# Rotary products, modulation and retention transposes at other places of the order, and the loads of an overflow branch on another queue

## The chip, the core and the metric

The kernel runs on one core of a Trainium2 chip. The metric is the device time of one execution in microseconds; a run gives it as the median of several executions. Beside the times there is one profiled execution, from which all rows of a trace below are taken.

## What is computed

The reference is a transformer of two blocks over 256 tokens of width 1024, all in float32. The first block is the one that the change touches: a layer with modulation, three branches and a mixture of experts.

```python
mod = (jax.nn.silu(c) @ ada_w + ada_b)[:, None, :]
sh1, sc1, gt1, sh2, sc2, gt2 = jnp.split(mod, 6, axis=-1)
h = rmsnorm(x, norm1_g) * (1.0 + sc1) + sh1
(aq, ak, av, iq, ik, iw, bq, bf, bi, bg, cq, ck, cv, cg, ga, gb, gc) = split_cols(h @ w_in)
o_a = dsa_attention(...)
o_b = hgrn2(...)
o_c = retention(cq, ck, cv, cg)     # 4 heads; rotated q and k, decay, then norm and silu(cg)
merged = (jax.nn.sigmoid(ga) * (o_a @ w_branch_a)
          + jax.nn.sigmoid(gb) * (o_b @ w_branch_b)
          + jax.nn.sigmoid(gc) * (o_c @ w_branch_c))
x = x + gt1 * (merged @ w_out)
h2 = rmsnorm(x, norm2_g) * (1.0 + sc2) + sh2
x = x + gt2 * hier_moe(h2, ...)     # 32 experts, two per token
```

The second block has feed-forward layers, a gated spatial unit and one attention layer; the change leaves them alone.

## The kernel before, in words

Each float32 weight matrix is streamed from HBM in units of 128 x 2048 numbers (1 MiB) and split into two halves that TensorE takes as fp32r: `wh` is the rounded weight (a cast on ScalarE, line 259) and `wl` the rest (a subtraction on VectorE, line 260), twice per unit, for 128 x 1024 numbers each. The activations are split in the same way (`hi`, `lo`), and each product is three matmuls (lines 280 to 282). `load_split` does this for one unit and counts the units in `nunit`. There are three staging tiles for weights and three split halves, so the splits run a unit or two ahead of the matmuls. `block_a` multiplies two or four units into two PSUM banks, in groups of 12 matmuls of 512 columns for each unit and token half; `unit_b` is the other orientation, with 48 matmuls of 256 columns.

At the end of `load_split` two kinds of other work are given a turn. From the sixth unit on, every third unit takes one job of `self.jobs`: a step of the later modulation. For each of four chunks (`ada_jobs`: scale and shift of the second norm, then the two gates) there were five steps: step u loads 1 MiB of `ada_w` into the one tile `adw` and weighs it on VectorE, adds up the columns of step u - 1 (`sum_rows`: two matmuls, line 650, and a VectorE add, line 651); the last step also calls `done` for the finished columns. For a gate, `done` is `ada_row`: a transpose (line 677), a copy and a DMA. And every unit advances `self.steps` by one, which was the generator of the second branch's decay.

`hybrid` is the layer up to the experts, in this order: projections, first branch, cq and ck (units 40 to 47), `decay_out` of the second branch, the rotations of cq and ck (six VectorE products or sums each, lines 1089 to 1094), cv (units 48 to 55), cg into `oc` (units 56 to 63), the retention scores, `branch(32)` for the second branch (units 64 to 71), `retention` for the two token halves with its 16 transposes of two column blocks each (`t_split`, line 453, in the four PSUM banks "mm"), one early expert load, and `branch(36)` for the third (units 72 to 83). Then four units of the output projection. `b8` hands out nine work tiles of 8 KiB per partition.

`experts` then runs 16 pairs of experts. Their weights, 192 units of 1 MiB, are loaded by SyncE (`load_slot`, line 1222) into 17 slots, most of which become free as the layer before ends; a slot is loaded again as soon as TensorE has used it (`both`, matmuls at line 1241). After the eighth pair stands `overflow`: each engine loads a count into a register and passes `tc.If(n > C)` (line 1456). Its body, a loop over all experts, is for tokens that found no place among the 64 of an expert. The measured input has none, so the body does not run.

All instructions are written in program order and then ordered by a planner, which runs a timing model and puts an instruction on its engine's queue when its inputs are ready by that model; each engine works its queue in order. `no_sync(later, earlier)` tells the planner only that one instruction stays behind another.

Of the kernel before, what the change touches and what calls it, by code (L numbers as in the profile page):

```python
# [8 lines left out]
F32 = mybir.dt.float32  # L9
# [175 lines left out]
class Program:  # L185
    def __init__(self, tc, d, out, dbg=None, cap_limit=CAP):
        self.tc, self.nc, self.d, self.out, self.dbgs = tc, tc.nc, d, out, dbg or {}
        self.cap_limit = cap_limit
        self.flip = 0
        self.nhalf = 0  # L190
        self.whx = None
        self.res = self.edge = self.rest = None
        self.nfront = FRONT
        self.ready = []
        self.ahead = []
        self.jobs = []
        self.behind = None
        self.steps = iter(())
        self.nunit = 0

    def pad(self, pool, n, name):
# [38 lines left out]
    def load_split(self, ap, kt, n=2048, o=0):  # L240

        nc = self.nc
        ws = self.stage(ap, n)
        m, per, w = n // 2, kt // 2, n // kt
        behind = self.behind
        if self.nfront < FRONT:
            behind = self.fronts.get(1)
            self.nfront += 1
        parts = []
        for i in range(2):  # L250
            j = self.nhalf % (WHL + WH2 if self.whx else WHL)
            if self.whx and j >= WHL:
                wh, wl = [self.whx.tile([128, 1088], F32R, name=nm, bufs=WH2)[:, o:o + 1024] for nm in ("whx", "wlx")]
            else:
                whl = self.whl(F32R, j == WHL - 1, o)
                wh, wl = whl[:, :1024], whl[:, 1024:]
            src = ws[:, i * m:i * m + m]
            self.nhalf += 1
            w1 = nc.scalar.copy(wh[:, :m], src)  # L259
            w2 = nc.vector.tensor_sub(wl[:, :m], src, wh[:, :m].bitcast(F32))  # L260
            for ins, other in zip((w1, w2), behind or ()):
                if other is not None:
                    self.no_sync(ins, other)
            self.last_split = w1, w2
            parts.append((wh, wl))

        self.nunit += 1
        if self.jobs and self.nunit >= ADA_FROM and self.nunit % ADA_EVERY == 0:
            self.jobs.pop(0)()
        next(self.steps, None)  # L270

        def get(k, c0=0, c1=w):
            a = (k % per) * w
            return tuple(p[:, a + c0:a + c1] for p in parts[k // per])

        return get
# [26 lines left out]
    def block_a(self, aps, hi, lo, mid=None, between=None):  # L303


        ps = self.mms(2)
        last = 4 * len(aps) - 1
        for i, ap in enumerate(aps):
            w = self.weights(ap, 4, o=BESIDE if hi is self.hi else 0)
            for t in range(2):  # L310
                ts = slice(t * 128, t * 128 + 128)
                for k in range(4):
                    kk = i * 4 + k
                    self.mm3(ps[t], hi[:, kk, ts], lo[:, kk, ts], *w(k), kk == 0, kk == last)
                if i == 0 and t == 0 and between is not None:
                    between()
            if i == 0 and mid is not None:
                mid()
        return ps
# [123 lines left out]

        return tile_of

    def t_split(self, src, hi, lo, n, gain=None):

        nc = self.nc
        for i in range(0, n, 2):
            ps = self.mms().rearrange("p (a b) -> p a b", a=2)  # L450
            for j in range(2):
                for t in range(2):
                    nc.tensor.transpose(ps[:, j, t * 128:t * 128 + 128], src(i + j, t), self.ident)
# [199 lines left out]
    def ada_jobs(self, chunk, done):  # L653
# [4 lines left out]
        accs = {}  # L658

        def step(u):  # L660
            if u:
                self.sum_rows(accs[u - 1], o, chunk, u - 1)
            if u == 4:
                done(o)
                return
            ws = self.mix.tile([128, 2048], F32, name="adw", bufs=1)
            nc.sync.dma_start(ws, self.d["ada"][chunk * 4 + u])
            accs[u] = self.small.tile([128, 256], F32, name="acc", bufs=3)
            self.weigh_sum(ws, accs[u])

        return [lambda u=u: step(u) for u in range(5)]

    def ada_row(self, chunk, o):

# [54 lines left out]
    def hybrid(self):  # L729
# [79 lines left out]
        self.gemm_b(18, 4, lambda u, ps: self.evac(cq[:, u], ps))  # L809
        self.gemm_b(22, 4, lambda u, ps: self.evac(ck[:, u], ps))  # L810
        obs = self.decay_out(att, bi, ob)
        cqr, ckr = self.rotate(cq), self.rotate(ck)
        cv = [self.b8([128, 2048], name="cv") for _ in range(2)]
        self.proj_a(12, 4, lambda t, b, ps: self.evac(cv[t][:, b * 512:b * 512 + 512], ps))
        oc = [self.b8([128, 2048], name="oc") for _ in range(2)]
        self.proj_a(20, 4, lambda t, b, ps: self.silu_to(oc[t][:, b * 512:b * 512 + 512], ps))
        at = self.retention_scores(cqr, ckr)
        self.branch(32, obs, 4, mg, False)
        ocs = self.retention(at, cv, oc)
        self.no_sync(self.load_slot(), self.last_mm)  # L820
        self.branch(36, ocs, 8, mg, False, nk=4)
        self.dbg("mg", mg)
        while self.jobs:
            self.jobs.pop(0)()
# [6 lines left out]
        self.residual(acc, self.gt1)  # L831
        self.dbg("x1", self.x)

    def proj_a(self, off, nb, store):
        for b in range(nb):
            ps = self.block_a([self.d["w_a"][off + 2 * b], self.d["w_a"][off + 2 * b + 1]], self.hi, self.lo)
            for t in range(2):
                store(t, b, ps[t])
# [3 lines left out]
        self.nc.scalar.activation(s, ps, AF.Sigmoid)  # L842
        self.nc.vector.tensor_mul(out, ps, s)

    def branch(self, goff, o, woff, mg, first, nk=2):

        nc, d = self.nc, self.d
        sg = self.b8([128, 2, 1024], name="sg")
        self.proj_a(goff, 2, lambda t, b, ps: nc.scalar.activation(sg[:, t, b * 512:b * 512 + 512], ps, AF.Sigmoid))
        for b in range(2):  # L850
            ps = self.block_a([d["w_br"][woff + nk * b + i] for i in range(nk)], o[0], o[1])
            c = slice(b * 512, b * 512 + 512)
# [228 lines left out]


    def rotate(self, a):
        nc = self.nc
        cos = self.kk["cos"][:, None, :].to_broadcast([128, CH, S])
        sin = self.kk["sin"][:, None, :].to_broadcast([128, CH, S])
        e, o = a[:, :, 0], a[:, :, 1]
        tmp = self.b8([128, 2, CH, S], name="rot")
        nc.vector.tensor_mul(tmp[:, 0], o, sin)
        nc.vector.tensor_mul(tmp[:, 1], e, sin)  # L1090
        nc.vector.tensor_mul(e, e, cos)
        nc.vector.tensor_sub(e, e, tmp[:, 0])
        nc.vector.tensor_mul(o, o, cos)
        nc.vector.tensor_add(o, o, tmp[:, 1])
        return a

    def retention_scores(self, q, k):
        nc = self.nc
# [9 lines left out]
            nc.vector.tensor_mul(at[:, h, 256:], ps[:, 256:], dec[:, h, :128])  # L1108
        return at

    def retention(self, at, v, oc):
        nc = self.nc
        out = [(self.b8([128, 8, S], F32R, name="och"), self.b8([128, 8, S], F32R, name="ocl")) for _ in range(2)]
        for t in range(2):
            ms = self.small.tile([128, CH], F32, name="msc", bufs=2)
            rs = self.small.tile([128, CH], F32, name="rsc", bufs=2)
            pss = []
            for h in range(CH):
                hc = slice(h * 512, h * 512 + 512)
                ps = self.psum.tile([128, 512], F32, name="bg", tag="bg", bufs=4)  # L1120
                pss.append(ps)
                if t == 0:
                    nc.tensor.matmul(ps, at[:, h, :128], v[0][:, hc], start=True, stop=True)
                else:
                    nc.tensor.matmul(ps, at[:, h, 128:256], v[0][:, hc], start=True, stop=False)
                    nc.tensor.matmul(ps, at[:, h, 256:], v[1][:, hc], start=False, stop=True)
                jk = self.small.tile([128, 512], F32, name="sqj", bufs=1)
                nc.scalar.activation(jk, ps, AF.Square, accum_out=ms[:, h:h + 1])
            nc.vector.tensor_scalar(ms, ms, 1.0 / 512, EPS, op0=OP.mult, op1=OP.add)
            nc.gpsimd.tensor_tensor(out=rs, in0=ms, in1=self.mhalf[:, :CH], op=OP.pow)  # L1130
            for h in range(CH):
                hc = slice(h * 512, h * 512 + 512)
                nc.vector.scalar_tensor_tensor(oc[t][:, hc], pss[h], rs[:, h:h + 1], oc[t][:, hc], op0=OP.mult, op1=OP.mult)
        for z in range(2):
            self.t_split(lambda c, t: oc[t][:, (8 * z + c) * 128:(8 * z + c) * 128 + 128], out[z][0], out[z][1], 8)
        self.dbg("och0", out[0][0].bitcast(F32))
        self.dbg("och1", out[1][0].bitcast(F32))
        return Cat(out[0][0], out[1][0]), Cat(out[0][1], out[1][1])


    def experts(self):
# [304 lines left out]
    def overflow(self, topi, rgs, iota):  # L1446
# [1 line left out]
        nc, d, tc, exs = self.nc, self.d, self.tc, self.exs  # L1448
        C = self.cap_limit
        n = nc.values_load(topi[0:1, 0:1], min_val=0, max_val=S)  # L1450
        rg = self.dram.tile([NE, 128, 4], F32, name="rgscr")

        def mm():
            return self.psum.tile([128, 512], F32, name="mm", tag="mm", bufs=4)

        with tc.If(n > C):
            nc.sync.dma_start(rg.rearrange("e p c -> p e c"), rgs)
            with tc.For_i(0, NE) as e:
                with tc.tile_pool(name="ov", bufs=1) as ov:
                    r = ov.tile([128, 4], F32, name="r")  # L1460
                    nc.sync.dma_start(r, rg[ds(e, 1)].rearrange("a p c -> p (a c)"))

                    def weight(u, c):
                        w = ov.tile([128, 512], F32, name="ows")
                        nc.sync.dma_start(w, d["w_e"][ds(e, 1), u, :, c:c + 512].rearrange("a p c -> (a p) c"))
                        return w

                    for c0 in range(C, S, 128):
# [411 lines left out]
```

## Time and profile before

| | us |
|---|---|
| median of three runs | 2094.13 (2090.36 to 2094.59) |
| the profiled execution | 2091.0 |
| its span | 2089.2 |
| TensorE busy | 2020.9 |
| VectorE busy | 1111.5 |
| ScalarE busy | 844.4 |
| GpSimd busy | 25.1 |

503 MB were moved, 241 GB/s over the span. The profile lists what each engine did and, before each instruction, how long its engine was idle and what ended that. A busy time does not tell what a stage is worth: one reads for each stretch of the span which engine is full, and whether the chain of waits that ends last runs through it.

### The profile page before, as it was taken

To read this page: it belongs to the slowest core of one execution; us is meant where nothing else is said; L and a number is where in the kernel's file an instruction comes from. 1 tells how busy PE (TensorE), PEld (TensorE's weight loads), DVE (VectorE), ACT (ScalarE), POOL (GpSimd) and SP (SyncE) were. 2 spreads that over 40 slices of the span, in tenths; PEclk is the share of its full clock that TensorE was granted. 3 is DMA by queue.
4 is the path that set the end of the run, shared out by engine and by line. 5 is a ranking of instruction groups with operands and counts; after the bars stand their busy time and mean duration, and the time that the engine had idled before them with its cause. 6 is when DMAs were issued, how large, how long until landed. Compare 5 with 4: busy or idle time off the path is not lost.

```text
span 2089.2 us, 29415 instructions
## 1 busy us (share of the span) xinstructions
PE 2020.9 (97%) x12256; PEld 1605.2 (77%) x12256; DVE 1111.5 (53%) x1596; ACT 844.4 (40%) x1200; POOL 25.1 (1%) x40
## 2 busy tenths in 40 slices
PE   7999999999999999898889999999999999999998
PEld 5889889778784444343339998879999999989997
DVE  5887876755552011010027556666556655586555
ACT  3454335344442211111116445445444644475443
POOL 0000000000000000000000000000000000000000
PEclk9999999999999999999999999999999999999999
DMA  8655445565588999999995556544555455434552
GB/s 326 239 202 208 181 161 205 188 235 196 184 351 325 421 421 421 381 421 421 421 374 208 183 189 227 200 150 173 188 196 183 173 191 182 162 121 159 184 187 96
DMA packets 72124, 503.17 MB, mean 241 GB/s; under 512 B 8218, under 2 KB 10034, under 8 KB 11698
## 3 DMA queue, kind: packets, MB, share of 16 engines
q1 hardware_dynamic: 71986, 501.24, 62.9%
q8 instruction: 98, 1.61, 0.3%
q14 instruction: 40, 0.33, 0.0%
HBM read 500.14 MB, written 1.07 MB: 240 GB/s over the span
## 4 chain that ended last, share of the span: by engine, by line
PE 45%; DMA 9%; DVE 2%; issue 1%; ACT 1%; POOLq 0%; SPq 0%; DVEq 0%; POOL 0%; ACTq 0%
PE mm L280 10%; PE mm L281 10%; PE mm L282 10%; PE bg L280 5%; PE bg L281 5%; PE bg L282 5%; DMA wx<-in_w_e 3%; DMA we<-in_w_e 3%; DMA whl<-in_w_e 2%; DMA wp<-in_w_e 1%; PE mm L1241 1%; PE mm L423 0%; DVE sn L1803 0%; PE mm L1832 0%; DVE whd L260 0%
## 5 line engine op out<-in xcount | busy, mean ns | idle before, releaser
L260 DVE TENSOR_TENSOR whl<-ws,whl 128x1024 fp32r<-128x1024 f32 x228 | 277.8, 1221 | 220.3 <-ACT whl L259 219.1
L259 ACT CAST whl<-ws 128x1024 fp32r<-128x1024 f32 x228 | 238.3, 1048 | 294.4 <-PE mm L282 247.7
L260 DVE TENSOR_TENSOR wlx<-ws,whx 128x1024 fp32r<-128x1024 f32 x165 | 201.1, 1222 | 139.1 <-ACT whx L259 138.3
L259 ACT CAST whx<-ws 128x1024 fp32r<-128x1024 f32 x165 | 172.5, 1050 | 172.5 <-PE mm L282 97.0
L280 PE MATMUL mm<-hi,whl 128*128 128x256 f32 x836 | 235.4, 282 | 1.1 <-DVE whl L260 1.0
L281 PE MATMUL mm<-lo,whl 128*128 128x256 f32 x836 | 233.9, 280 | 0.1
L282 PE MATMUL mm<-hi,whl 128*128 128x256 f32 x836 | 233.3, 279 | 0.0
L260 DVE TENSOR_TENSOR whd<-ws,whd 128x1024 fp32r<-128x1024 f32 x113 | 137.8, 1219 | 110.4 <-ACT whd L259 109.6
L259 ACT CAST whd<-ws 128x1024 fp32r<-128x1024 f32 x113 | 118.2, 1046 | 171.3 <-PE mm L282 126.2
L280 PE MATMUL mm<-hi,wlx 128*128 128x256 f32 x640 | 178.7, 279 | 0.5 <-ACT rrow L1597 0.5
L281 PE MATMUL mm<-lo,whx 128*128 128x256 f32 x640 | 178.5, 279 | 0.0
L282 PE MATMUL mm<-hi,whx 128*128 128x256 f32 x640 | 178.5, 279 | 0.0
L280 PEld LDWEIGHTS mm<-hi,whl 128*128 128x128 f32 x836 | 157.2, 188 | 3.2 <-issue 1.2
L281 PEld LDWEIGHTS mm<-lo,whl 128*128 128x128 f32 x836 | 157.2, 188 | 1.5 <-DVE lo L621 0.7
L282 PEld LDWEIGHTS mm<-hi,whl 128*128 128x128 f32 x836 | 157.2, 188 | 0.2
L1261 DVE TENSOR_TENSOR act<-act,mm 128x512 f32<-128x512 f32 x16 | 11.0, 688 | 242.1 <-PE mm L1241 242.1
L280 PEld LDWEIGHTS mm<-hi,wlx 128*128 128x128 f32 x640 | 120.3, 188 | 1.8 <-ACT rrow L1597 0.8
L281 PEld LDWEIGHTS mm<-lo,whx 128*128 128x128 f32 x640 | 120.3, 188 | 0.7
L282 PEld LDWEIGHTS mm<-hi,whx 128*128 128x128 f32 x640 | 120.3, 188 | 0.0
L281 PE MATMUL mm<-whl,hi 128*128 128x512 f32 (+1 forms) x304 | 115.4, 379 | 0.0
L282 PE MATMUL mm<-whl,hi 128*128 128x512 f32 (+1 forms) x304 | 114.0, 375 | 0.0
L280 PE MATMUL mm<-whl,lo 128*128 128x512 f32 (+1 forms) x304 | 112.1, 382 | 1.5 <-DVE lo L437 1.5
(560 smaller groups left out, 4235.4 us busy)
## 6 DMA issues: line engine op xcount, KB each, us to landing
ws<-in_w_fi SPq DMA_DIRECT2D x88, 1024.0 KB, 4.8
we<-in_w_e SPq DMA_DIRECT2D x79, 1024.0 KB, 19.8
wx<-in_w_e SPq DMA_DIRECT2D x44, 1024.0 KB, 19.8
ws<-in_w_fo SPq DMA_DIRECT2D x44, 1024.0 KB, 4.8
ws<-in_w_a SPq DMA_DIRECT2D x40, 1024.0 KB, 4.8
ws<-in_w_e SPq DMA_DIRECT2D x33, 1024.0 KB, 19.8
ws<-in_w_b SPq DMA_DIRECT2D x26, 1024.0 KB, 4.8
whl<-in_w_e SPq DMA_DIRECT2D x22, 1024.0 KB, 17.0
```

Of the source, the lines that this page charges most:

```text
L259: w1 = nc.scalar.copy(wh[:, :m], src)
L260: w2 = nc.vector.tensor_sub(wl[:, :m], src, wh[:, :m].bitcast(F32))
L280: first = mm(out, ll, rh, start=start, stop=False)
L281: mm(out, lh, rl, start=False, stop=False)
L282: self.last_mm = mm(out, lh, rh, start=False, stop=stop)
L1241: self.chain(self.pe, self.nc.tensor.matmul(ps[j * 64:j * 64 + 64], xs[:, k, j], ws[j][:, o:o + 512], start=(k == 0), stop=(k == last)))
L1261: V.tensor_mul(a, a, ps[1])
```

## The change

There are four parts. The rotations become a generator, given to `self.steps`: one of their twelve operations per unit, held behind the unit's last VectorE split, over the units of cv and oc. `ada_jobs` has six steps for each chunk: `done` is a step of its own, one job after the last sum. `retention` is called once for each token half, the first ahead of `branch(36)`, the second between the two blocks of that branch's gate projection, followed by the early expert load; the transposes are a generator, `self.turns`, which `block_a` advances after each group of 12 matmuls: two empty turns, two turns of two column pairs, four of one. They use the four PSUM banks "bg". And the loads in the body of the overflow branch are issued by GpSimd instead of SyncE, with their scratch table laid out by partition.

```diff
-        self.steps = iter(())
+        self.steps = self.turns = iter(())
...
-        next(self.steps, None)
+        if (step := next(self.steps, None)) is not None:
+            self.no_sync(step, self.last_split[1])
...
                 if i == 0 and t == 0 and between is not None:
                     between()
+                next(self.turns, None)
...
-    def t_split(self, src, hi, lo, n, gain=None):
+    def t_split(self, src, hi, lo, n, gain=None, tag="mm"):
...
-            ps = self.mms().rearrange("p (a b) -> p a b", a=2)
+            ps = self.mms(tag=tag).rearrange("p (a b) -> p a b", a=2)
...
         def step(u):
+            if u == 5:
+                done(o)
+                return
             if u:
                 self.sum_rows(accs[u - 1], o, chunk, u - 1)
             if u == 4:
-                done(o)
                 return
...
-        return [lambda u=u: step(u) for u in range(5)]
+        return [lambda u=u: step(u) for u in range(6)]
...
-        cqr, ckr = self.rotate(cq), self.rotate(ck)
+        self.steps = (s for a in (cq, ck) for s in self.rotate(a))
         cv = [self.b8([128, 2048], name="cv") for _ in range(2)]
...
-        at = self.retention_scores(cqr, ckr)
+        for _ in self.steps:
+            pass
+        at = self.retention_scores(cq, ck)
         self.branch(32, obs, 4, mg, False)
-        ocs = self.retention(at, cv, oc)
-        self.no_sync(self.load_slot(), self.last_mm)
-        self.branch(36, ocs, 8, mg, False, nk=4)
+        ocs = self.retention_out()
+        part = [lambda t=t: self.retention(t, at, cv, oc) for t in range(2)]
+        part[0]()
+
+        def second():
+            part[1]()
+            self.no_sync(self.load_slot(), self.last_mm)
+            self.turns = self.retention_turns(oc, ocs)
+
+        self.branch(36, (Cat(ocs[0][0], ocs[1][0]), Cat(ocs[0][1], ocs[1][1])), 8, mg, False, nk=4, mid=second)
...
-    def proj_a(self, off, nb, store):
+    def proj_a(self, off, nb, store, mid=None):
         for b in range(nb):
+            if b == 1 and mid is not None:
+                mid()
...
     def rotate(self, a):
...
-        nc.vector.tensor_mul(tmp[:, 0], o, sin)
+        yield V.tensor_mul(tmp[:, 0], o, sin)
...
+    def retention_turns(self, oc, out):
+
+        yield
+        yield
+        for i, n in ((0, 2), (2, 2), (4, 1), (5, 1), (6, 1), (7, 1)):
+            for g in range(i, i + n):
+                z, c = divmod(2 * g, 8)
+                self.t_split(lambda j, t: oc[t][:, (2 * g + j) * 128:(2 * g + j) * 128 + 128], out[z][0][:, c:c + 2], out[z][1][:, c:c + 2], 2, tag="bg")
+            yield
...
-        rg = self.dram.tile([NE, 128, 4], F32, name="rgscr")
+        rg = self.dram.tile([128, NE, 4], F32, name="rgscr")
...
         with tc.If(n > C):
-            nc.sync.dma_start(rg.rearrange("e p c -> p e c"), rgs)
+            nc.gpsimd.dma_start(rg, rgs)
...
-                    nc.sync.dma_start(r, rg[ds(e, 1)].rearrange("a p c -> p (a c)"))
+                    nc.gpsimd.dma_start(r, rg[:, ds(e, 1)].rearrange("p a c -> p (a c)"))
...
-                        nc.sync.dma_start(w, d["w_e"][ds(e, 1), u, :, c:c + 512].rearrange("a p c -> (a p) c"))
+                        nc.gpsimd.dma_start(w, d["w_e"][ds(e, 1), u, :, c:c + 512].rearrange("a p c -> (a p) c"))
```

## Rows read from the trace of the kernel before

**Rows 1.** The page: TensorE's busy time; DMA share in 40 equal slices.
```profile
PE 2020.9 (97%) x12256; PEld 1605.2 (77%) x12256; DVE 1111.5 (53%) x1596; ACT 844.4 (40%) x1200; POOL 25.1 (1%) x40
...
DMA  8655445565588999999995556544555455434552
```

**Rows 2.** Stretches: us; busy us (instructions) per engine; granted clock, DMA share, GB/s.
```profile
363.00:380.00 17.00, 13.49 (x86) 12.15 (x85) 16.34 (x19) 6.04 (x10) 0.00 (x0) 0.90 0.50 178
380.00:519.00 139.00, 139.00 (x608) 111.28 (x607) 84.20 (x103) 61.55 (x79) 2.02 (x2) 1.00 0.58 211
519.00:531.00 12.00, 10.06 (x58) 8.07 (x57) 9.78 (x14) 7.09 (x11) 0.00 (x0) 1.00 0.69 262
...
639.00:845.00 206.00, 204.55 (x1036) 91.30 (x1036) 22.79 (x44) 42.33 (x77) 0.00 (x0) 1.00 0.99 411
...
870.00:885.00 15.00, 14.27 (x78) 6.80 (x80) 2.49 (x5) 4.30 (x8) 0.00 (x0) 1.00 0.73 287
885.00:1072.00 187.00, 168.91 (x796) 69.59 (x792) 16.40 (x32) 27.99 (x51) 0.00 (x0) 1.00 1.01 421
```

**Rows 3.** The chain of waits, 878 to 1080 us: start, us, what.
```profile
882.89 9.38 DMA wx<-in_w_e
...
1052.34 19.81 DMA whl<-in_w_e
...
1072.19 3.65 PE mm L1241 x14
```

**Rows 4.** Timeline of TensorE, 369 to 380: start, us, instruction, count, [idle before].
```profile
369.80 0.50 PE L650 MATMUL mm<-ones,acc 128*128 128x1 f32 x4
373.81 0.27 PE L677 MATMUL mm<-k,ada 128*8 128x128 f32 x1 [3.51 <-DVE ada L651]
...
374.99 0.63 PE L281 MATMUL mm<-whl,hi 128*128 128x512 f32 x1
...
378.33 0.39 PE L280 MATMUL mm<-whl,lo 128*128 128x512 f32 x1
378.56 0.40 PE L281 MATMUL mm<-whl,hi 128*128 128x512 f32 x1
```

**Rows 5.** A stretch inside that timeline, columns as in rows 2.
```profile
374.00:379.00 5.00, 5.00 (x16) 3.94 (x16) 5.00 (x6) 0.26 (x1) 0.00 (x0) 0.66 0.62 211
```

**Rows 6.** Timeline of VectorE, 360 to 392.
```profile
370.74 1.22 DVE L1091 TENSOR_TENSOR cq<-cq,k 128x1024 f32<-128x1024 f32 x1
...
373.61 0.15 DVE L651 TENSOR_TENSOR ada<-mm,cc 128x2 f32<-128x2 f32 x1
```

**Rows 7.** Timeline of TensorE, 524 to 532.
```profile
526.91 0.66 PE L453 MATMUL mm<-k,oc 128*128 128x128 f32 x4 [0.33 <-DVE sg L857]
528.65 0.66 PE L453 MATMUL mm<-k,oc 128*128 128x128 f32 x4 [1.08 <-DVE ocl L345]
529.85 0.66 PE L453 MATMUL mm<-k,oc 128*128 128x128 f32 x4 [0.54 <-DVE ocl L345]
```

**Rows 8.** Timeline of TensorE and VectorE, end of the second half of the retention.
```profile
482.93 1.02 PE L1126 MATMUL bg<-cv,attc 128*128 128x512 f32 x2
...
486.00 2.73 DVE L1133 SCALAR_TENSOR_TENSOR oc<-bg,rsc,oc 128x512 f32<-128x512 f32 x4 [1.12 <-POOL rsc L1130]
```

**Rows 9.** Line 1456, the conditional: duration in ns (min/median/max), first and last start.
```profile
L1456 SPq EVENT_SEMAPHORE  x8: 17/17/17, 878.9 to 881.8; - x8
L1456 POOLq COMPARE_BRANCH  x1: 45/45/45, 635.0 to 635.0; - x1
...
L1456 PEldq COMPARE_BRANCH  x1: 5912/5912/5912, 845.6 to 845.6; - x1
...
L1456 SPq COMPARE_BRANCH  x1: 50/50/50, 861.9 to 861.9; - x1
```

**Rows 10.** Timeline of the SyncE queue, 419 to 460 and 840 to 892.
```profile
440.23 1.96 SPq L1222 DMA_DIRECT2D wx<-in_w_e  x4
...
861.50 21.76 SPq L1222 DMA_DIRECT2D wx<-in_w_e  x4
```

More of the change, by code (lines that the diff above doesn't have):

```diff
@@ L843, in silu_to, with branch @@
         self.nc.vector.tensor_mul(out, ps, s)
-    def branch(self, goff, o, woff, mg, first, nk=2):
+    def branch(self, goff, o, woff, mg, first, nk=2, mid=None):
         nc, d = self.nc, self.d
         sg = self.b8([128, 2, 1024], name="sg")
-        self.proj_a(goff, 2, lambda t, b, ps: nc.scalar.activation(sg[:, t, b * 512:b * 512 + 512], ps, AF.Sigmoid))
+        self.proj_a(goff, 2, lambda t, b, ps: nc.scalar.activation(sg[:, t, b * 512:b * 512 + 512], ps, AF.Sigmoid), mid)
         for b in range(2):
@@ L1083, in rotate @@
     def rotate(self, a):
-        nc = self.nc
+        V = self.nc.vector
         cos = self.kk["cos"][:, None, :].to_broadcast([128, CH, S])
@@ L1088, in rotate @@
         tmp = self.b8([128, 2, CH, S], name="rot")
-        nc.vector.tensor_mul(tmp[:, 0], o, sin)
[L1090 to L1095, printed above, removed]
+        yield V.tensor_mul(tmp[:, 0], o, sin)
+        yield V.tensor_mul(tmp[:, 1], e, sin)
+        yield V.tensor_mul(e, e, cos)
+        yield V.tensor_sub(e, e, tmp[:, 0])
+        yield V.tensor_mul(o, o, cos)
+        yield V.tensor_add(o, o, tmp[:, 1])
     def retention_scores(self, q, k):
@@ L1109, in retention_scores, with retention_out, retention @@
         return at
-    def retention(self, at, v, oc):
+    def retention_out(self):
+        return [(self.b8([128, 8, S], F32R, name="och"), self.b8([128, 8, S], F32R, name="ocl")) for _ in range(2)]
+    def retention(self, t, at, v, oc):
         nc = self.nc
[L1113 to L1138, printed above, removed]
@@ new lines, in retention @@
+        ms = self.small.tile([128, CH], F32, name="msc", bufs=2)
+        rs = self.small.tile([128, CH], F32, name="rsc", bufs=2)
+        pss = []
+        for h in range(CH):
+            hc = slice(h * 512, h * 512 + 512)
+            ps = self.psum.tile([128, 512], F32, name="bg", tag="bg", bufs=4)
+            pss.append(ps)
+            if t == 0:
+                nc.tensor.matmul(ps, at[:, h, :128], v[0][:, hc], start=True, stop=True)
+            else:
+                nc.tensor.matmul(ps, at[:, h, 128:256], v[0][:, hc], start=True, stop=False)
+                nc.tensor.matmul(ps, at[:, h, 256:], v[1][:, hc], start=False, stop=True)
+            jk = self.small.tile([128, 512], F32, name="sqj", bufs=1)
+            nc.scalar.activation(jk, ps, AF.Square, accum_out=ms[:, h:h + 1])
@@ new lines, in retention @@
+        nc.vector.tensor_scalar(ms, ms, 1.0 / 512, EPS, op0=OP.mult, op1=OP.add)
+        nc.gpsimd.tensor_tensor(out=rs, in0=ms, in1=self.mhalf[:, :CH], op=OP.pow)
+        for h in range(CH):
+            hc = slice(h * 512, h * 512 + 512)
+            nc.vector.scalar_tensor_tensor(oc[t][:, hc], pss[h], rs[:, h:h + 1], oc[t][:, hc], op0=OP.mult, op1=OP.mult)
+    def retention_turns(self, oc, out):
[6 more added lines that the diff above has]
+            yield
```

## The prediction

> **What bounds the kernel now.** The page comes first: TensorE (PE) is busy 97% of the span, and the DMA engines have one long saturated stretch in the middle [rows 1]. So two things can shorten the run: PE's own gaps, and the DMA stream where that is full. The table by stage says which counts where [rows 2]. Before the experts PE is busy without a break, but for 363 to 380 us (13.49 of 17) and 519 to 531 (10.06 of 12); the DMA engines have room there (share 0.50 to 0.69). From 639 us they are full (411 to 421 GB/s, share 0.99 to 1.01), and only one later stretch falls below that: 870 to 885 us, at 287 GB/s. The chain of waits agrees: from 882.89 to 1072.14 us it runs through expert weight loads alone, in links of about 19.8 us, and after them through PE [rows 3]. In the expert stage, then, a microsecond in which no load runs is lost to the end, and PE's idle time there is worth nothing (168.91 busy of 187). In the stage before it a microsecond that PE stands is lost too: the expert stage starts with the routing that PE's work ends in, and moves with it.
>
> The profiled execution took 2091.0 us (span 2089.2 and 1.8 around it); the median of the three timed runs is 2094.13, 3.1 more. The sum is made against 2091.0, and its difference is taken off 2094.13.
>
> **Part 1: the modulation a step later.** A chunk's last column sum (two matmuls, L650, and a VectorE (DVE) add, L651) and what is done with the finished columns stood in one step; now the second follows three weight units later. In the trace that join is the 3.51 us gap: the sums of the gate start at 369.80, and the transpose L677 waits until 373.81 [rows 4]. What it waits for is the add at 373.61; it is short, but DVE's queue is in order, and ahead of it stand rotations and splits of some 1.2 us each [rows 6]. The wait has a tail: eight matmuls start between 374.99 and 378.33, 0.42 us apart, and the next two are 0.23 apart [rows 4]; the granted clock from 374 to 379 was 0.66, a mix of the 1.2 and the 2.4 GHz level [rows 5]. The tail is worth 3.34 - 8 x 0.23 = 1.5 us. A unit here is 24 matmuls, 24 x 0.23 = 5.5 us, and three are 16.6 us, so an add that is late by four is over by then. **Gain 3.5 + 1.5 = 5.0 us** (bounds: 0, if the planner puts the transpose behind such a queue again, and 5.0). The step adds no instruction. The jobs now end at unit 75 instead of 63, of 83 before the output projection, so nothing is left over for the end. The staging tile of the modulation is last used at unit 69, not 60. Four expert loads wait for its pool; they were issued at 440.23 [rows 10] and move back by 9 units of 5.5 us, to about 490. The DMA engines have 0.42 of their time free there [rows 2], and the loads are not read before 639: cost nothing. Without that cover (a release as late as the output projection) they would fall into the full stretch, at 19.8/8 = 2.5 us each [rows 3], 10 us.
>
> **Part 2: rotations bound to splits.** The same twelve DVE operations of about 1.2 us go out one to a unit, each behind the split of its unit, over 12 of the 16 units of cv and oc. From 363 to 380 DVE is busy 16.34 of 17 us, from 380 to 519 84.20 of 139 [rows 2], so there is room: 1.2 us more in each unit of 5.5. No PE wait but the one above is removed by it, and the gain of part 1 is not counted twice. It costs something if a user now waits. The scores need all rotations; these end at unit 59 and the scores are wanted after unit 63, 22 us later. And the second rotation buffer holds one of nine work buffers until unit 59, so the second oc tile, first written after unit 57, can be late by about two units; the four PSUM banks of the blocks allow two blocks to stand. I take nothing; the bounds are 0 and one wait like that of rows 4, 3.5 us.
>
> **Part 3: retention spread.** Before, the transposes of all oc tiles stood in front of the last branch, and PE waited three times for a bank to be emptied by DVE: 0.33 + 1.08 + 0.54 = 1.95 us [rows 7]. Now they are cut into six turns, between the groups of 12 matmuls (2.7 us) of the last branch, and use the other four banks. The first turn lies behind three groups, 8.2 us. What must be over by then is the second half of the retention; in the trace, from its last matmul's end at 483.95 to the end of the scaling at 488.73, it took 4.8 us [rows 8], and the planner had it over 41 us before the last of the transposes (488.73 against 529.85). So the cover is 3.4 us longer than the chain. Each later pair has one group or more between its transposes and its reader. What is late next is a split on ScalarE or DVE between two turns. **Gain 1.95, less 0.5** for one small wait left; bounds of what is left are 0 and six waits of the longest kind seen, 6 x 1.08 = 6.5 us.
>
> **Part 4: overflow loads by GpSimd.** The conditional is not taken here: no instruction of its body is in the trace. What it costs stands at L1456 [rows 9]. SyncE (SP) branches at 861.9, then eight semaphore instructions follow, the first at 878.9 and the last at 881.8, and only then the next load: four loads that otherwise leave one behind the other take from 861.50 over 21.76 us [rows 10], the first ahead of the branch. At 421 GB/s a load of 1 MiB takes 2.5 us, so a link of 19.8 us is eight loads in flight; the one issued at 861.5 lands at 861.5 + 19.8 = 881.3. I read this as a queue that has to see all its loads landed before it passes the conditional, since the body it skips would use the same eight counters. GpSimd (POOL), which had no work in the body, branches at 635.0 and has no such instructions: that is what SP becomes. GpSimd gets the eight, with nothing in flight, and nobody waits for it in this stage. The DMA hole is (1 - 287/421) x 15 = 4.8 us [rows 2], in the stretch where the chain is DMA. PE's own branch (5.91 us [rows 9]) stays; it lies beside full DMA. **Gain 4.8 us** (bounds 0 and 4.8).
>
> The Trainium skill says otherwise of such a wait ("Runtime: NRT & Kernel Launch", section on instruction fetch mechanics): a taken branch whose target lies outside what has been fetched stands until a DMA has brought the target. PE's 5.91 us at its branch agrees with that; that SP's first semaphore comes 17 us after its branch could be the same. By that rule the hole is gone too if SP's part of the body shrinks, and stays if SP still jumps over loop code.
>
> **Sum.** 5.0 + 1.45 + 4.8 = 11.25, taken as 11.2: 2091.0 - 11.2 = 2079.8 for a run like the profiled one, 2094.1 - 11.2 = **2082.9** by the median. I take 2082, since the before runs lie 3.8 below that median at their lowest.
>
> **Rivals.**
> - The hole at the conditional stays (SP still has semaphores of its own there, or waits for code). For: the branch is still on every engine's path. Against: GpSimd's row. 2094.1 - 6.45 = 2087.7.
> - The turns wait: at each of the six PE stands 1.08 us for a late split. 2094.1 - 9.8 + 6.5 - 1.95 = 2088.9. For: ScalarE and DVE also split weights then. Against: 380 to 519 us shows both with time to spare [rows 2].
> - The change doesn't do what it says: the planner keeps its own order, and the transpose of the gate waits again elsewhere. 2094.1 - 6.2 = 2087.9. For: the order is the planner's, by modelled times that missed this wait once. Against: three units between.
> - **Slower.** The turns' waits become long enough to take PE to the 1.2 GHz level. Place: the second block of gc and the first of the last branch. Price: six groups of 12 matmuls at 0.42 instead of 0.23 us are 13.7 us, with six waits of 1.08 us 20.2: 2094.1 - 9.8 + 20.2 = 2104.5. It decides from 14 us of such losses on (9.8 of gains and 4.2 of uncertainty). Against: the waits of rows 7 left the clock at 1.00 in that stretch [rows 2]; only 3.5 us in one piece lowered it.
>
> **How the numbers follow.** Forecast 0.70, hole stays 0.10, turns wait 0.10, planner's order 0.05, slower 0.05. A measurement of this kernel can tell about 0.2% (4.2 us) from no change: the bound is 2089.9. Faster by more: most of the forecast, the hole and the planner's case, half of the turns' case, less something for a second cost among those taken as nothing (3.5 us): 0.83. Within: 0.11. Slower: 0.06. The range reaches down to 2077 (the forecast on a run as low as the lowest before, with all 11.75 gained, is 2078.6) and up to 2090, which takes in three rivals.
>
> **What would show it.** Right: no PE gap before L677; no L453 waits in a row in front of the last branch; twelve rotations one to a unit; no semaphores of SP at the conditional, GpSimd with eight, and 420 GB/s straight through it; the expert stage starting some 6 us earlier and ending some 11 earlier. Wrong: a new PE wait for DVE near the oc units, L453 waits in the turns, or a DMA hole of 4.8 us that has only moved.

## The result, and the profile after

The kernel after took 2080.02 us (median, 2079.64 to 2080.85), the one before 2092.67 in the same rounds: a ratio of 0.9941, 95% interval 0.9929 to 0.9952. The profiled execution took 2079.64 (span 2078.0), 11.36 less than the 2091.0 of before; the sum of the prediction was 11.25. The total is right. Its terms are not: by the traces one was some 2 us too large and one too small by half, one part taken as nothing was worth something, and about a microsecond of the difference is no work of the change.

Busy shares on the page hardly move. The page of the kernel after, busy time of each engine, TensorE (PE) first:

```profile
PE 2018.9 (97%) x12256; PEld 1607.8 (77%) x12256; DVE 1110.5 (53%) x1596; ACT 843.9 (41%) x1200; POOL 25.4 (1%) x40
```

PE did the same work in 2 us less of listed time, and stood about 9 us less (2078.0 - 2018.9 against 2089.2 - 2020.9 [rows 1]; an engine stands while it waits with nothing to run, and a stand is one such wait). The table by stage of the kernel after shows where (columns as in [rows 2]):

```profile
363.00:380.00 17.00, 17.00 (x99) 14.98 (x98) 14.98 (x21) 7.95 (x11) 0.00 (x0) 1.00 0.50 185
...
519.00:531.00 12.00, 12.00 (x55) 9.89 (x54) 7.70 (x10) 5.51 (x7) 0.00 (x0) 1.00 0.66 252
...
863.00:878.00 15.00, 15.00 (x82) 6.95 (x83) 1.81 (x4) 4.30 (x8) 0.00 (x0) 1.00 1.01 418
878.00:1061.00 183.00, 167.58 (x794) 69.34 (x792) 16.38 (x32) 27.99 (x51) 0.00 (x0) 1.00 1.01 421
```

The two gaps of PE are closed (17.00 of 17, 12.00 of 12, where [rows 2] had 13.49 and 10.06), the clock of the first stretch is 1.00 instead of 0.90, and the stretch that ran at 287 GB/s runs at 418. The conditional has moved to L1478; its rows answer to [rows 9]:

```profile
L1478 POOLq EVENT_SEMAPHORE  x4: 17/43/43, 628.8 to 629.0; - x4
L1478 POOLq COMPARE_BRANCH  x1: 45/45/45, 626.3 to 626.3; - x1
L1478 POOLq INC_SWDGE_SEM  x1: 166/166/166, 629.1 to 629.1; - x1
...
L1478 PEldq COMPARE_BRANCH  x1: 5932/5932/5932, 837.3 to 837.3; - x1
...
L1478 SPq COMPARE_BRANCH  x1: 50/50/50, 853.5 to 853.5; - x1
```

SyncE (SP) has only its branch left. GpSimd (POOL) has five instructions behind its own, four semaphores and one of another kind, where the prediction had eight. The chain of the kernel after, in order of time (start, us, what), answers to [rows 3]:

```profile
839.24 21.30 DMA we<-in_w_e
...
860.61 19.82 DMA wx<-in_w_e
...
1039.59 21.27 DMA whl<-in_w_e
...
1060.89 3.65 PE mm L1263 x14
```

It is still one of expert loads, with no short link in it (the one of 9.38 us at 882.89 in [rows 3] is a load issued behind the hole, with few others in flight). The last load of the chain lands 11.3 us earlier (1060.86 against 1072.15). But the last link is 21.27 us long, where before it was 19.81; that comes back below.

For the experiments the span is cut at three places which every kernel has. For before and after the first two are the first and the last line of these fences (duration in ns, then first and last start in us); the line between them, the transposes of the second branch's output, parts stage A once more:

```profile
L877 PE MATMUL bg<-biasr,k x8: 592/592/697, 84.8 to 87.9; 128*128 128x512 f32 x8
...
L453 PE MATMUL mm<-k,ob x16: 271/272/273, 363.9 to 369.7; 128*128 128x128 f32 x16
...
L453 PE MATMUL mm<-k,mg x16: 270/272/273, 580.1 to 603.7; 128*128 128x128 f32 x16
```

```profile
L892 PE MATMUL bg<-biasr,k x8: 592/592/697, 83.8 to 86.9; 128*128 128x512 f32 x8
...
L455 PE MATMUL mm<-k,ob x16: 271/272/273, 361.8 to 367.7; 128*128 128x128 f32 x16
...
L455 PE MATMUL mm<-k,mg x16: 270/272/273, 571.2 to 594.8; 128*128 128x128 f32 x16
```

A is from the first bias product to the first transpose of the merged branches (parts 1 to 3 lie in it), B from there to GpSimd's branch (routing), C from there to the end of the span (part 4). What lies ahead of A is not touched by the change; it varied from 83.5 to 85.6 us over the profiled runs. Each stage is read from one profiled execution. The last column is the median against that of the kernel before in the same rounds.

| kernel | start | A | B | C | median | against before |
|---|---|---|---|---|---|---|
| before | 84.8 | 495.3 | 54.9 | 1454.2 | | |
| after | 83.8 | 487.4 | 55.1 | 1451.7 | 2080.02 | -12.65 |
| after, again | 83.8 | 487.1 | 55.1 | 1451.7 | 2080.22 | -11.37 |
| without 1 | 83.5 | 491.4 | 56.8 | 1451.4 | 2084.76 | -6.83 |
| without 2 | 83.9 | 490.1 | 54.9 | 1451.4 | 2082.78 | -8.81 |
| without 1, 2 | 85.0 | 492.8 | 56.8 | 1453.0 | 2086.78 | -4.81 |
| without 3 | 83.9 | 492.7 | 55.0 | 1451.4 | 2086.24 | -5.90 |
| without 3, eight banks | 84.8 | 487.1 | 54.9 | 1451.4 | 2079.89 | -12.52 |
| without 4 | 85.2 | 487.2 | 55.0 | 1454.0 | 2083.16 | -8.98 |
| SP store, 8 pieces | 85.6 | 487.3 | 54.9 | 1455.6 | 2084.47 | -7.67 |
| SP store, 1 piece | 84.3 | 487.2 | 55.1 | 1451.8 | 2079.74 | -12.40 |
| 1 and 2 alone | 84.4 | 490.8 | 55.1 | 1456.6 | 2089.45 | -2.96 |
| 3 alone | 85.5 | 492.3 | 55.1 | 1454.2 | 2087.95 | -4.46 |
| 4 alone | 84.2 | 496.8 | 54.9 | 1452.5 | 2089.00 | -3.41 |

Stage A repeats to 0.3 us in the five kernels that have parts 1 to 3 whole (487.1 to 487.4; differences in A are taken against 487.3 unless another kernel is named). Where TensorE stands in it, it repeats less well: three pairs of other kernels have the same code in A, and these differ by 1.5 (before, and 4 alone), 1.9 (without 3, and 1 and 2 alone) and 0.5 us (without 1 and 2, and 3 alone). The kernel before ran from 2090.4 to 2094.6, and the intervals of the ratios are 0.0018 to 0.0030 wide, that is two to three us to either side. So neither the stages nor the medians alone decide a difference of 1 or 2 us; both are given where they differ.

Stage A has a part ahead of the waits that the prediction priced: from the first bias product to the first transpose of the second branch's output it is 278.7 to 279.3 us in the five kernels without part 1, and 277.8 to 278.5 in the nine with it. The rest of A is 216.2 us before and 209.4 after.

### The profile page after: what moved, and what is told of

The parts are those of the page before. It is cut to its first block, busy times and chain, and to the rows that moved or that the text cites. A ratio compares the mean times of both kernels' runs of the same rounds, so it can differ in the third digit from the quotient of the medians.

```text
span 2078.0 us, 29416 instructions
## 1 busy us (share of the span) xinstructions
PE 2018.9 (97%) x12256; PEld 1607.8 (77%) x12256; DVE 1110.5 (53%) x1596; ACT 843.9 (41%) x1200; POOL 25.4 (1%) x40
## 4 chain that ended last, share of the span: by engine, by line
PE 82%; DMA 13%; DVE 3%; ACT 1%; issue 1%; POOLq 0%; SPq 0%; DVEq 0%; POOL 0%; ACTq 0%
PE mm L281 17%; PE mm L282 16%; PE mm L283 16%; PE mm L1263 8%; PE bg L281 5%; PE bg L282 5%; PE bg L283 5%; DMA we<-in_w_e 4%; DMA wx<-in_w_e 4%; DMA whl<-in_w_e 2%; PE bg L1025 1%; DMA ws<-in_w_e 1%; DMA wp<-in_w_e 1%; PE mm L1198 1%; PE bg L581 1%
## 6 DMA issues: line engine op xcount, KB each, us to landing
we<-in_w_e SPq DMA_DIRECT2D x79, 1024.0 KB, 19.8
wx<-in_w_e SPq DMA_DIRECT2D x44, 1024.0 KB, 19.8
ws<-in_w_e SPq DMA_DIRECT2D x33, 1024.0 KB, 19.8
whl<-in_w_e SPq DMA_DIRECT2D x22, 1024.0 KB, 19.8
```

## Experiments

### Parts 1 and 2: the wait ahead of the gate's transpose

Without part 1:

```diff
-            if u == 5:
-                done(o)
-                return
             if u:
                 self.sum_rows(accs[u - 1], o, chunk, u - 1)
             if u == 4:
+                done(o)
                 return
...
-        return [lambda u=u: step(u) for u in range(6)]
+        return [lambda u=u: step(u) for u in range(5)]
```

> Part 1 undone, the rest of the changed kernel kept: the finished columns of the modulation are used in the same step as their last sum again; the rotations stay one to a unit. The changed kernel took 2080.0 us, the one before 2092.7. Theory A (the join was late only because dense rotations stood ahead of the add on VectorE; either edit alone removes that): no stand of TensorE over 1 us ahead of the gate's transpose, 2080 within 1 us. Theory B (the later step is what removes it, as the prediction put it: a split of about 1.2 us each still stands ahead of the add): the 3.5 us stand and up to 1.5 us of clock tail return, 2083.5 to 2085.

It took 2084.76 us, 4.5 more than the changed kernel in the same rounds, and A is 4.1 longer. The timeline of TensorE in that kernel:

```profile
371.29 0.27 PE L679 MATMUL mm<-k,ada 128*8 128x128 f32 x1 [2.02 <-DVE ada L653]
```

The stretch behind it (columns as in [rows 2]):

```profile
372.00:374.00 2.00, 2.00 (x7) 1.52 (x6) 1.97 (x4) 0.00 (x0) 0.00 (x0) 0.50 0.80 334
```

And the timeline of VectorE (DVE) ahead of the add:

```profile
368.20 1.23 DVE L260 TENSOR_TENSOR whd<-ws,whd 128x1024 fp32r<-128x1024 f32 x1 [1.83 <-ACT whd L259]
369.35 1.22 DVE L1103 TENSOR_TENSOR rot<-cq,k 128x1024 f32<-128x1024 f32 x1
370.48 0.68 DVE L358 COPY ck<-mm 128x512 f32<-128x512 f32 x1
371.08 0.15 DVE L653 TENSOR_TENSOR ada<-mm,cc 128x2 f32<-128x2 f32 x1
```

The wait is back, and shorter: one rotation and a copy stand between the split at 368.20 and the add, where in the kernel before two rotations (369.61 and 370.74), a split and a copy did. Behind it the clock is at 0.50, that is 1.2 GHz. (B is 1.7 us longer in this execution, at a mean clock of 0.88 from 611 to 640, where the kernel after has 0.94; that is not tied to part 1, since the kernels before, 3 alone and 4 alone lack it too and have 54.9 to 55.1.) So thinning out VectorE alone does not remove the join (theory A falls). Without part 2:

```diff
-        self.steps = (s for a in (cq, ck) for s in self.rotate(a))
+        for a in (cq, ck):
+            for _ in self.rotate(a):
+                pass
```

> Part 2 undone, the rest of the changed kernel kept: the twelve products and sums of the rotations stand together again ahead of the third projection; the modulation stays a step later. Theory A and theory B (the later step alone removes the wait at the gate's transpose): 2080 within 1 us. Rival C (twelve dense operations of 1.2 us, about 14.6 us of VectorE, make the weight splits behind them late, and TensorE stands for those): one or more stands of TensorE for VectorE between 360 and 385 us of 1 us or more in sum, 2081 to 2085.

2082.78 us, and A is 2.8 us longer than with all parts. No wait at the transpose, but two others, in TensorE's list of waits (line waited for: us in total, times, longest):

```profile
PE mm L282 <- DVE whd L260: 1.1, 1, 1.1
PE mm L282 <- DVE whl L260: 1.0, 1, 1.0
```

And the stretch in which they lie:

```profile
363.00:380.00 17.00, 15.06 (x90) 12.75 (x88) 17.00 (x20) 7.42 (x9) 0.00 (x0) 1.00 0.33 121
```

That is the rival: with dense rotations VectorE is busy 17.00 of 17 us, and now splits of weights come late. In the kernel before these waits did not show; as I read it (no run tests it by itself), the 3.5 us for which TensorE stood gave VectorE the time to catch up. With both parts undone (the two diffs together):

> Parts 1 and 2 undone together, parts 3 and 4 kept. Prediction's sum: the stand of 3.5 us ahead of the gate's transpose and the stretch of 1.5 us lost at 0.66 of the clock return, 2085.0. Theory A: u1 and u2 are both at 2080 and only this one is at 2085. Theory B: u1 is here too. Rival (the wait was an accident of the other parts' order): no stand, 2080.

2086.78 us: A is 5.5 longer than after, and the wait of 3.5 us is there again:

```profile
PE mm L679 <- DVE ada L653: 3.5, 1, 3.5
```

Undone together they cost 5.5 in A, 4.2 of it behind the transposes of the second branch's output (213.6 against 209.4), where the wait lies; from there part 1 alone brings 2.7 and part 2 alone 1.4 (4.0 and 2.0 by the medians). (The profiled execution with both undone is the longest of nine, 2.5 us over their median; what it has over is in B and C.) So neither is the other's spare: they work on one queue. One thing the runs do not separate: with six steps to a chunk the gate's own last sum also comes later (its add at 394.20, the transpose at 415.9 in the kernel after), out of the stretch in which it waited.

> The changed kernel unaltered, timed in the same rounds as the three kernels with parts undone, so that differences of 1 to 5 us can be told: 2080, that is 0.9941 of the kernel before (interval so far 0.9929 to 0.9952). In its trace the stages up to 84 units should begin where they did: the expert stage 8.4 us earlier than in the kernel before, its last load 11.3 us earlier.

It did (2080.22; A 487.1).

### Part 3: other banks or other places

```diff
-        def second():
-            part[1]()
...
+        part[1]()
+        for z in range(2):
+            self.t_split(lambda c, t: oc[t][:, ...], ocs[z][0], ocs[z][1], 8)
+        self.no_sync(self.load_slot(), self.last_mm)
-        self.branch(36, ..., nk=4, mid=second)
+        self.branch(36, ..., nk=4)
```

> Part 3 undone, the rest of the changed kernel kept: both halves of the retention and all 16 transposes stand ahead of the last branch again and use the first four banks. Prediction's sum: TensorE stands for VectorE between the transposes, 1.95 us in three pieces before, so the expert stage starts 1.5 to 2 us later and the time is 2082. Rival (the stands are made up for elsewhere, or the turns cost as much): the expert stage starts at the same time, 2080 within 0.7 us.

2086.24 us, and 5.4 us more in A: neither forecast's number. The timeline of TensorE without part 3:

```profile
522.43 1.97 PE L455 MATMUL mm<-k,oc 128*128 128x128 f32 x8 [2.28 <-DVE ocl L347]
...
525.48 0.63 PE L282 MATMUL mm<-whl,hi 128*128 128x512 f32 x1
525.90 0.63 PE L283 MATMUL mm<-whl,hi 128*128 128x512 f32 x1
```

And a stretch of it:

```profile
523.00:527.00 4.00, 4.00 (x16) 3.61 (x15) 2.61 (x5) 1.17 (x2) 0.00 (x0) 0.50 0.02 8
```

The three short waits of [rows 7] have become one of 2.28 us, and the clock behind it is at 1.2 GHz: matmuls start 0.42 us apart, and the eight transposes take 1.97 us. Whether the place of the transposes or the banks matter was tried with the transposes written at that same place, and both sets of banks in turn:

```diff
-            self.t_split(lambda c, t: oc[t][:, ...], ocs[z][0], ocs[z][1], 8)
+            for c in range(0, 8, 2):
+                self.t_split(lambda j, t: oc[t][:, ...], ocs[z][0][:, c:c + 2], ocs[z][1][:, c:c + 2], 2, tag=("mm", "bg")[c // 2 % 2])
```

> As the kernel with part 3 undone (all transposes ahead of the last branch), but the pairs of columns take the banks mm and bg by turns, eight instead of four. That kernel took 2086.2 us, with a stand of 2.28 us behind 16 transposes and ten matmuls 0.43 us apart behind it. Theory B (TensorE waits for a bank to be emptied; other banks alone are enough, the spreading is not needed): no stand, 2080 to 2081. Theory P (it waits for VectorE's queue whatever the bank, so only spreading helps): the stand and the tail stay, 2085 to 2087.

2079.89 us, as fast as the changed kernel. Its transposes, from TensorE's timeline:

```profile
520.21 0.60 PE L455 MATMUL mm<-k,oc 128*128 128x128 f32 x4
520.65 0.38 PE L455 MATMUL bg<-k,oc 128*128 128x128 f32 x2
520.87 0.60 PE L455 MATMUL mm<-k,oc 128*128 128x128 f32 x4
521.30 0.60 PE L455 MATMUL bg<-k,oc 128*128 128x128 f32 x4
```

And the stretch around them:

```profile
519.00:531.00 12.00, 12.00 (x63) 10.16 (x63) 8.85 (x13) 5.49 (x8) 0.00 (x0) 1.00 0.36 138
```

No wait. TensorE waited for a bank to be emptied, and a second set of banks is enough; the turns between the groups of the last branch are not needed for it. (The order on the queue is not quite the same: with eight banks the planner put 16 of the 32 transposes into the first group, at 513.2 to 514.8 us, where without part 3 it had put eight. How much of the gain is that was not tried apart.)

### Part 4: what SyncE waits for at the conditional

```diff
-            nc.gpsimd.dma_start(rg, rgs)
+            nc.sync.dma_start(rg.rearrange("e p c -> p e c"), rgs)
...
-                        nc.gpsimd.dma_start(w, ...)
+                        nc.sync.dma_start(w, ...)
```

> Part 4 undone, the rest of the changed kernel kept: the loads in the body of the conditional, which does not run, are issued by SyncE again. Prediction's sum: SyncE gets eight semaphore instructions some 17 us after its branch, the load behind it is issued about 20 us after the one ahead of it, the DMA rate falls below 300 GB/s for about 15 us, and 4.4 to 4.8 us come back: 2084.4 to 2084.8. Rival (the hole costs nothing since TensorE's work is what ends last): 2080 within 0.7 us, hole in the trace all the same.

2083.16 us. (The scratch table has its old layout again here; the next two kernels keep the new one.) Without part 4 the row of SP at the conditional, its queue's timeline, the stretch behind it, and two links of the chain, each in a fence of its own:

```profile
L1478 SPq EVENT_SEMAPHORE  x8: 17/17/17, 871.2 to 874.1; - x8
```

```profile
853.73 21.81 SPq L1244 DMA_DIRECT2D wx<-in_w_e  x4
```

```profile
863.00:878.00 15.00, 14.11 (x78) 6.51 (x76) 2.50 (x5) 4.30 (x8) 0.00 (x0) 1.00 0.73 288
```

```profile
884.48 20.70 DMA we<-in_w_e
...
1044.60 19.81 DMA whl<-in_w_e
```

Wait and hole are as predicted. The price is less by the trace, 2.3 us in C; by the medians it is 3.1 against the kernel after. Then the two readings of the wait. SP's part of the body is a short store, with no loop, in eight transfers or in one:

```diff
-            nc.gpsimd.dma_start(rg, rgs)
+            for g in range(0, NE, 4):
+                nc.sync.dma_start(rg[:, g:g + 4], rgs[:, g:g + 4])
```

> The changed kernel, but the store of the scratch table in the body of the conditional is issued by SyncE in eight pieces; the loads of the body's loop stay with GpSimd, so SyncE's part of the body is short and has no loop. The body does not run. Drain theory (a queue that passes a conditional whose body uses its counters has to see the eight loads in flight landed): eight semaphore instructions of SyncE, the first about 17 us after its branch, a DMA hole of 4.4 to 4.8 us, 2084.4 to 2084.8. Fetch theory (the time went into fetching code that lies far away): no stand and no hole with such a short body, 2080 within 0.7 us. The Trainium skill (Runtime: NRT & Kernel Launch, instruction fetch mechanics) would give the second.

2084.47 us. The first three views again, with eight transfers:

```profile
L1478 SPq EVENT_SEMAPHORE  x8: 17/17/17, 871.5 to 874.4; - x8
...
L1478 SPq COMPARE_BRANCH  x1: 45/45/45, 854.5 to 854.5; - x1
```

```profile
854.12 21.68 SPq L1244 DMA_DIRECT2D wx<-in_w_e  x4
```

```profile
863.00:878.00 15.00, 14.15 (x76) 6.55 (x74) 2.50 (x5) 4.30 (x8) 0.00 (x0) 1.00 0.73 291
```

```diff
-            nc.gpsimd.dma_start(rg, rgs)
+            nc.sync.dma_start(rg, rgs)
```

> As the kernel with eight pieces, but the store of the scratch table is one transfer of SyncE, so one counter of the eight is used in the body. The body does not run. Drain theory: one semaphore instruction of SyncE, which waits for the one load on that counter alone: if that is the oldest of the eight in flight, about 2.5 us, the time of one load at 421 GB/s, and no hole, 2080 to 2080.7; if it is the youngest, about 17 us and a hole as with eight. Fetch theory: no stand, 2080 within 0.7 us.

2079.74 us. The same three with one transfer:

```profile
L1478 SPq COMPARE_BRANCH  x1: 50/50/50, 853.6 to 853.6; - x1
L1478 SPq EVENT_SEMAPHORE  x1: 17/17/17, 855.7 to 855.7; - x1
```

```profile
853.27 10.37 SPq L1244 DMA_DIRECT2D wx<-in_w_e  x4
```

```profile
863.00:878.00 15.00, 14.15 (x76) 6.50 (x74) 2.51 (x5) 4.30 (x8) 0.00 (x0) 1.00 1.01 419
```

Eight transfers in a body that never runs bring back eight semaphores, 17 us of wait and the hole; one transfer brings one semaphore, 2.1 us behind the branch, and no hole. Loads leave every 2.5 us and take 19.8, so 17 us fits the drain of all eight in flight, and 2.1 us that of the oldest. By these three kernels what counts is how many transfers of SP the body holds, not the length of its code: eight short transfers cost the same wait as the loop of loads. Nor is it the layout of the scratch table, which is the new one in both.

The rule of the Trainium skill which the prediction set against this reading ("Runtime: NRT & Kernel Launch", instruction fetch mechanics) gives no stand for so short a body, if that lies within what has been fetched, which no row shows; the row with eight transfers, beside the one with a single transfer, speaks against it for SP. PE's 5.9 us at its branch stay in all kernels (5.91 to 6.21 us); no run here tells whether that is the fetch.

### Each part alone

The kernel before with one part made, composed of the diffs above.

> Parts 1 and 2 alone (parts 3 and 4 undone). With all four parts the kernel took 2080.0 to 2080.2 us, the one before 2091.6 to 2092.7. Theory S (the parts add up; undoing parts 1 and 2 cost 6.6 us by the medians, 4.3 by the stage from the transposes of the second branch's output to those of the merged branches, 216.2 us before): 2085.5 to 2088, that stage 211.9. Theory I (they don't: with parts 1 and 2 the transposes ahead of the last branch come with one stand of 2.28 us and a slow clock behind it, as in the kernel with part 3 alone undone, where before there were three short ones): the stage about 214.9, 2088.5 to 2090.

A is 4.5 us shorter than before. The stand of 2.28 us is there, as theory I has it, but without a slow clock behind it in this execution. TensorE's timeline and the same stretch:

```profile
523.60 1.25 PE L455 MATMUL mm<-k,oc 128*128 128x128 f32 x8 [2.28 <-DVE ocl L347]
```

```profile
523.00:527.00 4.00, 3.40 (x19) 2.69 (x20) 3.60 (x7) 1.17 (x2) 0.00 (x0) 1.00 0.13 55
```

The stage that the theories name is 212.3 us, close to theory S (211.9); the median (2089.45) agrees with theory I. So this run does not decide between them. C is 2.4 us longer than before in the profiled run; an expert load near the end (`whl`) is issued 417.6 us behind GpSimd's branch, against 417.3 before, so the other 2 us lie later, behind the experts for the most part, and I can't say why.

> Part 3 alone (parts 1, 2 and 4 undone). Theory S (undoing part 3 cost 6.1 us by the medians, so doing it alone gives as much): 2086. Theory I (without the other parts only the three stands of rows 7 are there to be removed, and the stage goes from 216.2 to 213.6, as the kernel with parts 1 and 2 undone showed): 2089 to 2090. In both the stand of 3.5 us ahead of the gate's transpose is there.

3.0 us in A, 4.5 by the medians: between the two theories. Theory I's stage is met (213.6), with a median a microsecond better. Of the 3.0, 1.95 are the three stands and 0.4 lies ahead of the second branch's transposes; the rest was not located.

> Part 4 alone (parts 1 to 3 undone). Prediction's sum: 4.8 us less than the kernel before, 2087.2. By the traces so far (from the conditional of GpSimd to the landing of the last expert load 437.15 us before, 434.56 after, 437.01 with part 4 undone, since the stream without the hole has a link of 21.1 to 21.3 us near its end where the one with the hole has 19.8): 2.4 to 2.6 us less, 2089.3 to 2089.7, with that long link in the chain. If the long link is tied to the place and not to the missing hole: no such link and 2088.

2089.00 us, 3.4 less than before, and the long link is in its chain, as the second forecast had it:

```profile
1048.90 21.07 DMA whl<-in_w_e
```

C gains 1.7; from GpSimd's branch to the landing of the chain's last expert load it is 1069.97 - 635.9 = 434.1 against 437.15, a gain of 3.1. A is 1.5 longer than before: the three short waits of [rows 7] are the same, but this time they left a slow clock (0.70 from 531 to 535).

## Why the prediction was right, term by term

**Part 1 and part 2**: forecast 5.0 + 0, measured 5.5 in A with part 3 made, 4.5 without it. That the size is right is in part luck: the stretch with the wait gives 4.2 (216.2 - 212.3 = 3.9 without part 3), and the rest lies ahead of it in A, where the prediction had nothing and no wait of TensorE was removed; it goes with part 1, and its cause was not located. The split between the parts is wrong. "No PE wait but the one above is removed by it" was true of the trace of before and wrong as a step: without part 2 two waits of 1.10 and 1.02 us take the place of the one removed, so part 2 is worth 2.8 us beside part 1. The bound given for part 2 looked only at what it might cost. That the gate's join only moves three units was also too simple, as said above. The four expert loads moved from 440.23 to 465.61, half as far as the 490 forecast, and cost nothing.

**Part 3**: forecast 1.45, measured 3.0 alone and 5.4 beside the others (3.6 in the execution without the slow clock, 1 and 2 alone against without 4). The term took the waits as they stood in [rows 7]; but these depend on what VectorE has queued, and in both kernels that have parts 1 and 2 without part 3 they are one of 2.28 us, behind which the clock fell in one execution of the two. The 0.5 held back for a wait in the turns did not come. The mechanism (a bank to be emptied) was right; what removes it is the second set of banks.

**Part 4**: forecast 4.8, measured 2.5 in C between before and after, 2.3 undone and 1.7 alone; by the medians 3.1 undone and 3.4 alone (the eight short transfers cost 4.5 over the kernel after). C holds the rest of the kernel too, which varied by up to 2 us. From GpSimd's branch to the landing of the chain's last expert load the kernels with the hole take 436.9 to 437.4 us (four profiled runs), those without 434.1 to 434.7 (eight); the chains of the other two, without 3 and 1 and 2 alone, end with another load. Cause and hole were right. The step that was too simple is that "a microsecond in which no load runs is lost to the end": near the end of the stream a part is given back. With no hole the chain has one link of 21.1 to 21.3 us there (nine profiled runs), with the hole it has 19.7 to 19.8 (five); behind the hole a link of 20.6 to 21.2 stands in four of those five. The SyncE queue of the kernel after and of the one without part 4:

```profile
1044.56 0.33 SPq L1244 DMA_DIRECT2D wp<-in_w_e  x1
1048.48 2.82 SPq L1244 DMA_DIRECT2D we<-in_w_e  x2
```

```profile
1049.55 0.33 SPq L1244 DMA_DIRECT2D wp<-in_w_e  x1
1052.03 2.82 SPq L1244 DMA_DIRECT2D we<-in_w_e  x2
```

Counted from GpSimd's branch (626.3 and 627.4), the load of `wp` goes out 3.9 us earlier without the hole (418.3 against 422.2), the next one only 2.4 us earlier (422.2 against 424.6): it waits 3.5 us for a load to land, 1.4 us longer than its neighbours do, while the rate stays at 416 to 421 GB/s. So 3.9 of the 4.8 us stood up to there, and 1.4 went in one late landing. Why it is late is open; it was not tried.

**The sum**: 7.9 in A and 2.5 in C, less 0.2 in B, make 10.2; the other microsecond lies ahead of A, in code that the change leaves alone, and varies as much from run to run. So 11.25 was met by a part 4 that was 2.3 too large, parts 1 to 3 that were 1.45 too small (7.9 against 6.45), and 1.0 of chance. Of the 7.9, 6.8 lie in the stretch with the waits that were priced (216.2 - 209.4) and 1.1 ahead of it. The errors cancel; that the total came out within about 0.1 us of the profiled difference (11.36) is luck.

**What would show it**: all points of the list came true but two, the number of GpSimd's semaphores and the start of the expert stage, forecast 6 and found 8.4 to 8.7 us earlier. The rivals fell: no hole, no wait in the turns, no slow clock in them, and the gate's transpose waits nowhere else.

## What to carry to other kernels

A conditional whose body issues transfers made the issuing queue wait for its transfers in flight even though the body was skipped (17 us with eight transfers in the body): give the body to an idle queue, or keep it to one transfer (2.1 us here; by the trace it waited for the oldest load, and a wait for the youngest was not seen). Before a gap is priced, ask what the engine that ends it has queued besides; a gap can hide the next one, and two edits on one queue must be priced together. And where TensorE waits for an evacuation, the copy that empties a bank, first try a second set of banks, then a new order.

## What the runs showed of the hardware

TensorE's clock after a stand is not settled by the instructions. In the profiled executions the same order with the same 2.28 us stand left 0.50 in one kernel (without 3) and 1.00 in another (1 and 2 alone); the three short stands of [rows 7] (1.95 us in sum) left 1.00 before and 0.70 with part 4 alone. Stands of 2.0 and 3.5 us were followed by the lower clock in each trace that has one; the two of 1.1 and 1.0 us, nine us apart, were not. Removing stands of about 2 us in sum was therefore worth from 3.0 us of stage A (3 alone) to 5.4 (part 3 beside the others), and a forecast should carry both ends.
